# Later modulation vectors as row sums of transposed weights

## The chip, the cores and the metric

The kernel runs on one core of a Trainium2 chip. The core has a matrix engine (TensorE, PE in the profile, with PEld for its weight loads), a vector engine (VectorE, DVE), a scalar engine (ScalarE, ACT), a general engine (GpSimd, POOL) and a queue engine (SyncE, SP) that issues the DMAs here. Time is device microseconds (us) from the first to the last instruction of an execution; lower is better. The kernel before took 1167.83 us in the median of three runs (1166.76 to 1171.36).

## The reference, cut to what matters

A trunk of two layers over 256 latent tokens and 256 context tokens, 1024 wide, in fp32. Each layer mixes tokens (a gated convolution branch beside windowed attention, gated, summed and projected) and then channels (a gated MLP with a short convolution). Both sub-layers are modulated by vectors that depend only on a conditioning vector, one for the latents (`c`) and one for the context (`c_ctx`):

```python
s_lat = jax.nn.silu(c)
s_ctx = jax.nn.silu(c_ctx)
for l in range(DEPTH):
    mod = (s_lat @ w_ada[l] + b_ada[l])[:, None, :]
    sh1, sc1, g1, sh2, sc2, g2 = jnp.split(mod, 6, axis=-1)
    mod_c = s_ctx @ w_ada[l] + b_ada[l]
    ...
    h = modulate(rmsnorm(x, norm1_g[l]), sh1, sc1)
    ...
    x = x + g1 * gated_merge(...)
    h2 = modulate(rmsnorm(x, norm2_g[l]), sh2, sc2)
    x = x + g2 * conv_ffn(h2, ...)
```

`w_ada[l]` has 1024 rows and 6144 columns, 24 MB a layer in fp32. In column tiles of 128 there are 48 a layer: tiles 0 to 7 are the first shift, 8 to 15 the first scale, 16 to 23 the first gate, then the second shift, scale and gate. Both streams need layer 0's tiles and layer 1's first two parts; of layer 1's later 32 tiles only the latents' half is needed, since the context stream ends there.

## The kernel before

Activations stand with channels on the partitions and tokens along the row (`x[k]`, eight tiles of 128 by 512, latents then context). Weights come in units of 128 by 1024 fp32 (512 KB), fetched by SP into a raw buffer (tag `raw`, four in turn, shared by main weights and modulation weights). A main weight unit is split into two fp32r parts that add up to it: ScalarE writes the high part (line 148), VectorE the low part (line 149); each has four buffers. A product of one unit is three TensorE passes per 128 rows (lines 167 to 169, `mm3`). An output tile of 128 by 512 in PSUM is 24 such products in layer 0 for the 1024-row weights, 12 for the 512-row branch weights.

The order of the work is the order in which the program calls it, engine by engine, and a planner may let an instruction that is ready go ahead of one that is not. Work that is not on the main line of products is written as generators: `add_side` enters one into a list, and `slot()`, called in the middle and at the end of each output tile (`group`, lines 171 to 179), advances each of them by one step. Generators in the list are the convolution's taps (line 521), the attention's steps, the layer norm (`layer_norm`), the norms (`norm`), and the making of modulation vectors.

These vectors are made in three ways before the change:

- `ada_now` (line 273): layer 0's first shift and scale, tile by tile at the start, by `ada_products` (line 188): TensorE takes `sil` (silu of both conditioning vectors, padded to 32 columns) as its stationary side and the raw unit as the moving one, 16 matmul records for two units (line 194), with the sums of the four row tiles on four groups of PSUM rows; ScalarE copies them to `ev` (line 202), TensorE transposes them (line 209), VectorE sums them and adds the bias (lines 211, 213).
- `ada_all` (line 215): the same for seven chunks of two column tiles of layer 0, tiles 16 to 29.
- `ada_vector` (line 227): the rest. VectorE multiplies each row tile of a raw unit by the channel's conditioning value and adds it to an accumulator `acc` (lines 257, 259); after eight row tiles TensorE transposes the accumulator in four pieces (line 236), and VectorE sums along the row (line 242) and adds the bias (line 243). Chunks hold two column tiles for both streams (16 VectorE instructions of 256 columns) or four for the latents alone (eight of 512 columns).

They run as side work in this order: `g1` from the end of layer 0's attention on (the five `ada_vector` chunks of tiles 30 to 39, then the seven `ada_all` chunks), which must be done before the second norm of layer 0; `ada_rest` in layer 0's up-projection (tiles 40 to 47, then layer 1's tiles 16 to 47 for the latents); `ad` in layer 0's down-projection (layer 1's tiles 0 to 15 for both streams). Nothing of it runs in layer 1.

Around `g1` the main line is: gate tiles (`gate`, one unit of 24 products each, evacuated by ScalarE), the attention's output branch (line 786, VectorE multiplies with the gates), the convolution's output branch (lines 790 to 793, VectorE forms the gated sum `z` in two parts), and the output projection (`U_WO`), which reads all eight tiles of `z`. The layer norm of the convolution branch runs beside it as side work; GpSimd does two of its additions (lines 747, 748).

At the start TensorE runs products that nobody reads (`busy`, line 123) until the inputs are there. In layer 0's first stage, up to about 62 us, value and gated-linear products alternate with `ada_now` for the next row tile.

Of the kernel before, what the change touches and what calls it, by code (L numbers as in the profile page):

```python
# [8 lines left out]
F32 = mybir.dt.float32  # L9
# [26 lines left out]
# places of the weight units of a layer: [128 rows, 1024] each  # L36
# [8 lines left out]
def trunk(ctx: ExitStack, tc: tile.TileContext, xt, cvec, wall, wada, params, bias_t, rope_t, out):  # L45
# [22 lines left out]
    def tmp(w=512):  # L68
        return tp.tile([P, w], F32, tag="t", bufs=5, name=nm("t"))
# [45 lines left out]
    sil = cp.tile([P, KD, 32], F32, name="sil")  # L115
# [3 lines left out]
    # TensorE's clock is at its full rate once it has been busy for a while: products for nobody until the inputs are there  # L119
# [5 lines left out]
    busy(28)  # L125
# [5 lines left out]
    lastdma = [None]  # L131

    def raw_unit(src):
        r = wp.tile([P, UW], F32, tag="raw", bufs=4, name=nm("raw"))
        lastdma[0] = sp.dma_start(r, src)
        return r

    def wparts(l, u, at=None, cuts=2):
        """The two parts of a unit: their sum is the unit, exactly. The first cut is split, the others by the call."""
        r = wp.tile([P, UW], F32, tag="raw", bufs=4, name=nm("raw"))  # L140
# [30 lines left out]
    def group(ps, ws, xh, xl, c):  # L171
        """One output tile: the sum over the row tiles ws."""
# [27 lines left out]
    def ada_rows(ps):  # L200
        ev = tp.tile([P, S], F32, tag="ev", name=nm("ev"))
# [3 lines left out]
    def ada_sums(l, j, ev):  # L205
        n = slice(j, j + 9, 8) if l == 0 and j < 8 else slice(2 * j, 2 * j + 2)
# [8 lines left out]
    def ada_all(chunks):  # L215
        late = None
        for l, j in chunks:
            ps = ada_products(l, j, "sc")
            if late:
                ada_sums(*late)  # L220
            late = (l, j, ada_rows(ps))
            yield
            yield
        yield
        ada_sums(*late)

    def ada_vector(chunks):
        """Products and sums over the row tiles on the vector engine: chunks of four column tiles for the latents
        alone, or of two for both streams, in steps of so many row tiles."""
        late = None  # L230
        left = 0

        def sums(l, n, m, acc):
            pt = psum("pt")
            for i in range(4):
                pe.transpose(sl(pt, i), sl(acc, i), ident)  # L236
            if m.shape[1] == 4:
                pv, b = pt.rearrange("p (i k) -> p i k", i=4), pr(l, BADA + n, 4)
            else:
                pv = pt.rearrange("p (s i k) -> p i s k", s=2, i=2)  # L240
                b = pr(l, BADA + n, 2).unsqueeze(2).to_broadcast([P, 2, 2])
            dve.tensor_reduce(m, pv, AX.X, ALU.add)
            dve.tensor_tensor(m, m, b, ALU.add)

        for l, j, both, step in chunks:
            acc = tp.tile([P, 512], F32, tag="acc", bufs=2, name=nm("acc"))
            per = 4 if both else 2
            r = None
            for k in range(KD):
                if k % per == 0:  # L250
                    r = raw_unit(wada[l, (8 * j + k) // per])
                i = k % per
                for s in range(1 + both):
# [826 lines left out]
```

## Time and profile before

| quantity | value |
|---|---|
| runs | 1171.36, 1167.83, 1166.76 us (median 1167.83) |
| profiled execution: span | 1167.3 us; its own time is this span, the page gives nothing around it |
| granted TensorE clock | 0.993 on average |
| busy: TensorE, weight loads | 1147.8 us, 984.5 us |
| busy: VectorE, ScalarE, GpSimd | 955.3 us, 555.5 us, 21.3 us |
| fetched from HBM | 185.47 MB |

Lines of groups read: line of the program, engine, operation, what it writes and reads with buffer numbers left out, sizes, count; then the total busy time and the mean in ns of one; then the engine's idle time just before them with what ended it. A busy TensorE is not TensorE at its peak, as its matmuls overlap: the time from one to the next is shorter than the duration of one. Lines of a timeline begin with the start and the duration in us; `xN` behind them merges N in a row. Lines of waits are the waiting engine and line, what it waited for, and then the total in us, the number and the longest. A line of windows is a stretch of the execution with each engine's busy time in it.

### The profile page before, as it was taken

To read this page: it belongs to the slowest core of one execution; us is meant where nothing else is said; L and a number is where in the kernel's file an instruction comes from. 1 tells how busy PE (TensorE), PEld (TensorE's weight loads), DVE (VectorE), ACT (ScalarE), POOL (GpSimd) and SP (SyncE) were. 2 spreads that over 40 slices of the span, in tenths; PEclk is the share of its full clock that TensorE was granted. 3 is DMA by queue.
4 is the path that set the end of the run, shared out by engine and by line. 5 is a ranking of instruction groups with operands and counts; after the bars stand their busy time and mean duration, and the time that the engine had idled before them with its cause. 6 is when DMAs were issued, how large, how long until landed. Compare 5 with 4: busy or idle time off the path is not lost.

```text
span 1167.3 us, 18318 instructions
## 1 busy us (share of the span) xinstructions
PE 1147.8 (98%) x6958; PEld 984.5 (84%) x6958; DVE 955.3 (82%) x1794; ACT 555.5 (48%) x914; POOL 21.3 (2%) x25
## 2 busy tenths in 40 slices
PE   8999999999999999999999999999999999999997
PEld 7677777878679978888888888989788999999997
DVE  4589999979765899898988688789888799988753
ACT  4346767323243444433443222444566667666542
POOL 0000000000000000000000000000000000000000
PEclk9999999999999999999999999999999999999998
DMA  7964434452771354766754346555756364665651
GB/s 270 322 175 131 116 95 120 157 156 69 244 236 55 109 166 159 234 214 221 221 179 151 122 165 209 160 182 187 182 154 165 133 216 140 207 193 185 185 189 55
DMA packets 60248, 199.25 MB, mean 171 GB/s; under 512 B 7168, under 2 KB 8192, under 8 KB 60160
## 3 DMA queue, kind: packets, MB, share of 16 engines
q1 hardware_dynamic: 60160, 198.08, 54.1%
q8 instruction: 55, 0.90, 0.3%
q14 instruction: 33, 0.27, 0.1%
HBM read 185.47 MB, written 1.05 MB: 160 GB/s over the span
## 4 chain that ended last, share of the span: by engine, by line
PE 75%; issue 17%; DMA 3%; DVE 2%; ACT 1%; POOL 0%; SPq 0%; POOLq 0%; DVEq 0%; ACTq 0%
PE main L167 20%; PE main L169 20%; PE main L168 20%; PE po L472 2%; DMA raw<-in_wall 1%; DMA ks<-qk 1%; PE main L573 1%; PE main L575 1%; PE main L574 1%; PE pt L453 1%; PE pt L236 1%; PE sc L167 1%; PE sc L169 1%; PE sc L168 1%; PE pt L334 1%
## 5 line engine op out<-in xcount | busy, mean ns | idle before, releaser
L167 PE MATMUL main<-h,whi 128*128 128x256 f32 (+1 forms) x1328 | 450.9, 340 | 0.9 <-ACT whi L148 0.9
L169 PE MATMUL main<-h,wlo 128*128 128x256 f32 (+1 forms) x1328 | 446.4, 336 | 0.1
L168 PE MATMUL main<-h,whi 128*128 128x256 f32 (+1 forms) x1328 | 444.7, 335 | 0.0
L148 ACT CAST whi<-raw 128x1024 fp32r<-128x1024 f32 (+1 forms) x247 | 255.0, 1035 | 355.9 <-PE main L168 189.2
L149 DVE TENSOR_TENSOR wlo<-raw,whi 128x1024 fp32r<-128x1024 f32 (+1 forms) x247 | 296.5, 1204 | 81.2 <-ACT whi L148 80.0
L167 PEld LDWEIGHTS main<-h,whi 128*128 128x128 f32 x1328 | 250.9, 189 | 31.7 <-issue 4.5
L169 PEld LDWEIGHTS main<-h,wlo 128*128 128x128 f32 x1328 | 251.0, 189 | 28.4 <-DVE wlo L149 0.7
L168 PEld LDWEIGHTS main<-h,whi 128*128 128x128 f32 x1328 | 251.3, 189 | 27.4 <-issue 0.6
L259 DVE SCALAR_TENSOR_TENSOR acc<-raw,sil,acc 128x256 f32<-128x256 f32 (+1 forms) x294 | 141.8, 530 | 1.1
L521 DVE SCALAR_TENSOR_TENSOR cb<-u,par,cb 128x512 f32<-128x512 f32 (+1 forms) x240 | 142.0, 619 | 0.6
L167 PE MATMUL main<-fh,whi 128*128 128x256 f32 (+1 forms) x396 | 127.2, 321 | 0.0
L169 PE MATMUL main<-fh,wlo 128*128 128x256 f32 (+1 forms) x396 | 126.4, 319 | 0.0
L168 PE MATMUL main<-fl,whi 128*128 128x256 f32 (+1 forms) x396 | 126.4, 319 | 0.0
L169 PEld LDWEIGHTS main<-fh,wlo 128*128 128x128 f32 x396 | 74.5, 188 | 5.9
L168 PEld LDWEIGHTS main<-fl,whi 128*128 128x128 f32 x396 | 74.5, 188 | 5.7
L167 PEld LDWEIGHTS main<-fh,whi 128*128 128x128 f32 x396 | 74.5, 188 | 5.7
L858 ACT ACTIVATE t<-main,par 128x512 f32<-128x512 f32 (+1 forms) x82 | 50.7, 667 | 13.6 <-PE main L169 13.5
L859 DVE SCALAR_TENSOR_TENSOR t<-main,par,t 128x510 f32<-128x510 f32 (+1 forms) x82 | 47.5, 614 | 1.9 <-ACT t L858 1.5
L862 DVE SCALAR_TENSOR_TENSOR t<-main,par,t 128x510 f32<-128x510 f32 (+1 forms) x82 | 46.8, 611 | 0.0
L798 DVE SCALAR_TENSOR_TENSOR x<-main,mod,x 128x256 f32<-128x256 f32 x48 | 22.2, 481 | 27.3 <-PE main L169 27.2
L358 ACT ACTIVATE h<-t,mod 128x256 fp32r<-128x256 f32 x56 | 25.3, 501 | 37.1 <-DVE t L357 37.0
L877 ACT CAST fh<-t 128x512 fp32r<-128x512 f32 (+1 forms) x44 | 22.5, 513 | 32.4 <-DVE t L874 31.7
(162 smaller groups left out, 1284.7 us busy)
## 6 DMA issues: line engine op xcount, KB each, us to landing
raw<-in_wall SPq DMA_DIRECT2D x239, 512.0 KB, 4.2
raw<-in_wada SPq DMA_DIRECT2D x96, 512.0 KB, 4.3
ks<-qk SPq DMA_DIRECT2D x32, 256.0 KB, 5.0
bias<-in_bias_t SPq DMA_DIRECT2D x8, 512.0 KB, 4.4
x<-in_xt SPq DMA_DIRECT2D x8, 256.0 KB, 3.9
raw<-in_wall SPq DMA_DIRECT2D x8, 256.0 KB, 5.9
qs<-qk SPq DMA_DIRECT2D x16, 128.0 KB, 2.4
rope<-in_rope_t SPq DMA_DIRECT2D x2, 512.0 KB, 6.0
```

Of the source, the lines that this page charges most:

```text
L148: act.copy(hi[:, c], r[:, c])
L149: dve.tensor_tensor(lo[:, c], r[:, c], hi[:, c].bitcast(F32), ALU.subtract)
L167: pe.matmul(ps, w[0], xh, start=start, stop=False)
L168: pe.matmul(ps, w[0], xl, start=False, stop=False)
L169: pe.matmul(ps, w[1], xh, start=False, stop=stop)
L259: dve.scalar_tensor_tensor(a, w, c, a, ALU.mult, ALU.add)
L358: act.activation(hi[:, c], y[:, c], AF.Identity, bias=b)
L472: pe.matmul(po[i * HD : (i + 1) * HD, c], self.V[kt][:, h * HD : (h + 1) * HD], pts[i][:, kt - kts[0], :], start=kt == kts[0], stop=kt == ...
L521: dve.scalar_tensor_tensor(cb[j], src, w, cb[j], ALU.mult, ALU.add)
L858: act.activation(c, pv_, AF.Identity, bias=pr(l, FDB + t, 1), scale=w[1])
L859: dve.scalar_tensor_tensor(c[:, :, 1:], pv_[:, :, : S - 1], w[0], c[:, :, 1:], ALU.mult, ALU.add)
L862: dve.scalar_tensor_tensor(c[:, :, : S - 1], pv_[:, :, 1:], w[2], c[:, :, : S - 1], ALU.mult, ALU.add)
```

## The change

All later modulation vectors (every tile but layer 0's first 16) are made in one way, `ada_dots`. The weights of these tiles are handed over transposed: a unit is one column tile, its 128 columns on the partitions and all 1024 rows along the row. The conditioning vectors are needed along the row, the same on every partition: at the start TensorE transposes each `sil` column, broadcast to 128 columns, into PSUM (16 transposes, four banks), and VectorE copies the four banks into two tiles `sb[0]` (latents) and `sb[1]` (context), behind the first norm's mean. Then a modulation value is a row sum of a product:

- for the latents, one VectorE instruction over 1024 columns multiplies the raw tile by `sb[0]` and gives the sum (`accum_out`); it writes the product over the raw tile;
- for the context (48 of the 80 tiles), GpSimd multiplies the raw tile by `sb[1]` into `pj` (one buffer), and a ScalarE copy of `pj` with a sum gives the value;
- one small VectorE instruction adds the bias to the tile before (`shift`).

A tile takes two steps of side work: fetch and GpSimd in the first, ScalarE and VectorE in the second. The transposes of accumulators, the accumulators, `ada_all` and `ada_vector` are gone; `ada_now` stays. The 96 fetches of 512 KB stay.

Memory is moved for `sb` and `pj`: the `t` tiles go from five to four, `acc` and `ev` go, `sil` moves into the pool of layer 0's first half, and the raw buffers go from four to three; in layer 1 every fourth raw tile is taken from an extra one-buffer pool in each half, so that there are four again. The banks that receive the broadcast vectors are those that the value products then use.

```diff
-        return tp.tile([P, w], F32, tag="t", bufs=5, name=nm("t"))
+        return tp.tile([P, w], F32, tag="t", bufs=4, name=nm("t"))
...
-    busy(28)
+    busy(8)
+
+    sb = [cp.tile([P, D], F32, name=f"sb{i}") for i in range(2)]
+    across = [psum() for _ in range(4)]
+    for i in range(4):
+        for k in range(4):
+            kk = 4 * (i % 2) + k
+            pe.transpose(sl(across[i], k), sil[:, kk, i // 2 : i // 2 + 1].to_broadcast([P, P]), ident)
+    busy(20)
...
+    def raw_tile():
+        raws[0] += 1
+        if raw_pools and raws[0] % 4 == 0:
+            return raw_pools[-1].tile([P, UW], F32, tag="raw", name=nm("raw"))
+        return wp.tile([P, UW], F32, tag="raw", bufs=3, name=nm("raw"))
...
-    def ada_all(chunks):
...
-    def ada_vector(chunks):
...
+    def shift(l, n, ns):
+        m = mods[l][:, n, :ns]
+        dve.tensor_tensor(m, m, pr(l, BADA + n, 1).to_broadcast([P, ns]), ALU.add)
+
+    def ada_dots(l, tiles, steps):
         late = None
+        for n, both in tiles:
+            r = raw_unit(wada[l, n])
+            if both:
+                pj = tp.tile([P, UW], F32, tag="pj", name=nm("pj"))
+                pool.tensor_tensor(pj, r, sb[1], ALU.mult)
+            yield
+            if late:
+                shift(*late)
+            if both:
+                act.activation(pj, pj, AF.Copy, accum_out=mods[l][:, n, 1:2])
+            dve.scalar_tensor_tensor(r, r, 1.0, sb[0], ALU.mult, ALU.mult, accum_out=mods[l][:, n, 0:1])
+            late = (l, n, 1 + both)
+            for _ in range(steps - 1):
+                yield
         yield
+        shift(*late)
...
                     mid = next(sums)
+                    with tc.issue_after(mid.ins):
+                        for i in range(4):
+                            dve.tensor_copy(sb[i // 2][:, (i % 2) * 512 : (i % 2 + 1) * 512], across[i])
                     nxt = ada_now(0)
...
-                        yield from ada_vector([(0, j, True, 1) for j in range(15, 20)])
-                        yield from ada_all([(0, j) for j in range(8, 15)])
-
-                    g1 = ada_more()
+                    g1 = ada_dots(0, [(n, True) for n in range(16, 40)], 2)
...
-                    yield from ada_vector([
-                        *((0, j, True, 1.3) for j in range(20, 24)),
-                        *((1, j, False, 1.5) for j in range(4, 12)),
-                    ])
+                    yield from ada_dots(0, [(n, True) for n in range(40, 48)], 2)
+                    yield from ada_dots(1, [(n, False) for n in range(16, 48)], 2)
...
-                ad = ada_vector([(1, j, True, 2) for j in range(0, 8)])
+                ad = ada_dots(1, [(n, True) for n in range(0, 16)], 2)
...
-    u = w.reshape(DEPTH, 2, 4, P, 24, S).transpose(0, 4, 1, 3, 2, 5).reshape(DEPTH, 48, P, UW).copy()
+    u = np.ascontiguousarray(w.transpose(0, 2, 1)).reshape(DEPTH, 48, P, UW).copy()
     u[0, :16] = w[0][:, : 2 * D].reshape(2, 4, P, 2, 8, P).transpose(4, 0, 2, 1, 3, 5).reshape(16, P, UW)
-    u[1, 16:] = w[1][:, 2 * D :].reshape(4, 2, P, 8, 512).transpose(3, 0, 2, 1, 4).reshape(32, P, UW)
```

More of the change, by code (lines that the diff above doesn't have):

```diff
@@ L114, in trunk @@
     dve.memset(mhalf, -0.5)
-    sil = cp.tile([P, KD, 32], F32, name="sil")
+    sil = ea0.tile([P, KD, 32], F32, name="sil")
     dve.memset(sil, 0.0)
@@ L227, in ada_vector @@
-    def ada_vector(chunks):
[L230 to L253, printed above, removed]
-                    w = r[:, i * UW // per : (i + 1) * UW // per]
-                    a, c = acc[:, s * S : (s + 1) * S] if both else acc, sil[:, k, s : s + 1]
-                    if k == 0:
-                        dve.tensor_scalar_mul(a, w, c)
-                    else:
-                        dve.scalar_tensor_tensor(a, w, c, a, ALU.mult, ALU.add)
-                left += 1
-                if left >= step:
-                    left -= step
-                    yield
-                    if late and k >= 2:
-                        sums(*late)
-                        late = None
-            n = 2 * j if both else 4 * j
-            late = l, n, mods[l][:, n : n + 2, :] if both else mods[l][:, n : n + 4, 0], acc
-        yield
-        yield
-        sums(*late)
```

35 lines of the change are left out of this document (18 added, 17 removed).

## The prediction

> **What bounds the kernel now.** I read first the page's busy shares, then a table of windows of the profile, then the single rows of the operations that the change touches.
>
> ```profile
> span 1167.3 us, 18318 instructions
> PE 1147.8 (98%) x6958; PEld 984.5 (84%) x6958; DVE 955.3 (82%) x1794; ACT 555.5 (48%) x914; POOL 21.3 (2%) x25
> ```
>
> TensorE is never idle for long, so time that is taken off it comes off the end, as long as the engines that feed it keep up. The feeder to watch is VectorE (DVE): it makes the low part of each weight unit (line 149). The windows show where it has room (after the stretch, each engine's busy time and instructions, the granted clock, the DMA share, GB/s):
>
> ```profile
> core 0: us, PE busy (x) PEld busy (x) DVE busy (x) ACT busy (x) POOL busy (x), PEclk, DMA share, GB/s
> 20.00:62.00 42.00, 40.84 (x256) 27.56 (x254) 23.80 (x59) 16.48 (x32) 0.00 (x0) 1.00 0.89 311
> 189.00:325.00 136.00, 135.09 (x683) 104.83 (x681) 117.19 (x220) 51.26 (x85) 3.35 (x2) 1.00 0.46 145
> 275.00:300.00 25.00, 25.00 (x113) 20.27 (x112) 24.37 (x46) 7.96 (x11) 0.00 (x0) 1.00 0.33 104
> 300.00:325.00 25.00, 24.09 (x163) 15.81 (x162) 17.05 (x39) 7.37 (x13) 0.00 (x0) 1.00 0.80 269
> 440.00:500.00 60.00, 60.00 (x268) 48.63 (x267) 55.68 (x91) 24.30 (x32) 0.00 (x0) 1.00 0.59 193
> ...
> PEld main L169 <- DVE wlo L149: 1.4, 2, 1.0
> ```
>
> From 189 to 325 us, where layer 0's 24 later modulation tiles for both streams are made, VectorE is busy 117.2 of 136 us, and from 275 to 300 it is full. The last line is from the waits of the weight loads between 189 and 345 us: twice they already waited for VectorE's low part, so its lead over TensorE does run out here. This stretch decides the case.
>
> **What TensorE loses.** Each of the 25 VectorE chunks ended in four transposes; seven more chunks were TensorE products. The first two lines are from the chain of waits, the count from the groups, the rest from the timeline of PE:
>
> ```profile
> 235.15 0.23 PE main L169
> ...
> 240.96 0.44 PE pt L236 x4
> ...
> L236 PE MATMUL pt<-ident,acc 128*128 128x128 f32 x100 | 15.0, 272 | 0.0
> ...
> 307.05 0.39 PE L169 MATMUL main<-sh,wlo 128*128 128x512 f32 x1
> 307.37 1.07 PE L194 MATMUL sc<-raw,sil 128*32 128x256 f32 x16
> 308.37 0.44 PE L209 MATMUL pt<-ident,ev 128*128 128x128 f32 x2
> 308.56 0.48 PE L167 MATMUL main<-sh,whi 128*128 128x512 f32 x1
> ```
>
> The 100 transposes are 25 x 0.44 = 11.0 us on the chain. A product chunk takes TensorE from 307.05 to 308.56, less the 0.23 us that a main product has on the chain: 1.28 us, seven times 9.0. Together **20.0 us**. The 16 new transposes at the start lie where nobody needs TensorE: its warming products end at 10.53 and the first real one begins at 10.85 (rows below), and as many warming products stay as fit.
>
> **What VectorE gets.** Per tile now one multiply with row sum over 1024 columns and one small addition of the bias.
>
> ```profile
> L259 DVE SCALAR_TENSOR_TENSOR acc<-raw,sil,acc 128x256 f32<-128x256 f32 x238 | 99.8, 478 | 0.0
> L259 DVE SCALAR_TENSOR_TENSOR acc<-raw,sil,acc 128x512 f32<-128x512 f32 x56 | 42.0, 750 | 1.1
> L243 DVE TENSOR_TENSOR mod<-mod,par 128x4 f32<-128x4 f32 x25 | 3.9, 156 | 0.0
> L418 ACT ACTIVATION_READ_ACCUMULATOR pp<-sc,mx 128x1 f32 x32 | 6.4, 199 | 0.0
> ...
> 249.00 2.85 DVE L259 SCALAR_TENSOR_TENSOR acc<-raw,sil,acc 128x256 f32<-128x256 f32 x7
> ...
> 189.00:325.00 136.00, 3.27 (x10) 1.00 0.46 145
> 189.00:325.00 136.00, 30.47 (x70) 1.00 0.46 145
> 189.00:325.00 136.00, 3.44 (x5) 1.00 0.46 145
> ```
>
> 256 more columns cost 272 ns, so 1024 last 750 + 2 x 272 = 1.29 us; in a row seven instructions of 0.478 take 2.85 us, so each overlaps the next by (3.35 - 2.85) / 6 = 0.08, leaving 1.21. The addition of 0.156 leaves 0.07. A row sum on VectorE is not in this trace; the nearest row is ScalarE's read of its accumulator, 0.20 us, of which some 0.1 is left by the same overlap. Below it could be nothing; above, the case of half rate among the rivals. I take **1.38 us per tile**. The last three lines are what lines 257, 259 and 242 cost VectorE from 189 to 325: 37.2 us go away there, 24 x 1.38 = 33.1 come. By this alone VectorE would need 117.2 - 37.2 + 33.1 = 113.1 us, and TensorE, which loses five transposed chunks (2.2) and five product chunks (6.4) here, 127.4: room of 14.3 us.
>
> **What GpSimd's multiply costs VectorE.** The context stream is multiplied by GpSimd, 48 times 128x1024, and summed by ScalarE. GpSimd now does two such additions a layer, and VectorE's rows beside them show the price (lines of POOL and of DVE, by time; last, the usual duration of line 521):
>
> ```profile
> 165.70 1.51 POOL L747 TENSOR_TENSOR ss<-cb,cb 128x512 f32<-128x512 f32 x1 [151.60 <-DVE cb L521]
> 166.59 1.17 DVE L521 SCALAR_TENSOR_TENSOR cb<-u,par,cb 128x512 f32<-128x512 f32 x1
> ...
> 203.53 2.15 POOL L748 TENSOR_TENSOR ss<-ss,cb 128x512 f32<-128x512 f32 x1 [36.32 <-DVE cb L521]
> 204.44 1.78 DVE L521 SCALAR_TENSOR_TENSOR cb<-u,par,cb 128x512 f32<-128x512 f32 x1
> ...
> 819.80 1.59 POOL L747 TENSOR_TENSOR ss<-cb,cb 128x256 f32<-128x256 f32 x1 [54.59 <-DVE cb L521]
> 820.71 0.97 DVE L521 SCALAR_TENSOR_TENSOR cb<-u,par,cb 128x256 f32<-128x256 f32 x1
> ...
> 866.61 1.99 POOL L748 TENSOR_TENSOR ss<-ss,cb 128x256 f32<-128x256 f32 x1 [45.22 <-DVE cb L521]
> 867.92 0.42 DVE L650 TENSOR_TENSOR t<-main,rope 128x256 f32<-128x256 f32 x1
> ...
> L521 DVE SCALAR_TENSOR_TENSOR cb<-u,par,cb 128x512 f32<-128x512 f32 x120 | 88.9, 755 | 0.1
> L521 DVE SCALAR_TENSOR_TENSOR cb<-u,par,cb 128x256 f32<-128x256 f32 x120 | 53.1, 483 | 0.4
> ```
>
> Beside 512 columns on GpSimd the instruction of VectorE took 1.78 instead of 0.75, beside 256 columns 0.97 instead of 0.48: it stood for 1.03 and 0.49 us. So 1024 columns would hold VectorE 1.03 + 2 x 0.54 = **2.1 us**. It isn't always paid: 0.42 us at 166.59, nothing at 867.92, where VectorE read PSUM. Of the four holds (3.04 us) 1.94 were paid, 64%. Bounds: nothing (all fall beside PSUM reads or idle time) and all. I take 64%, 1.35 us per tile, since the stretch mixes convolution taps (two SBUF inputs) with PSUM readers.
>
> [...]
>
> In the stretch VectorE then needs 113.1 + 24 x 1.35 = 145.5 us against 127.4: **18.1 us** by which TensorE must wait: behind the row sum, which overwrites the raw tile and so waits for GpSimd, stand VectorE's low parts of weights and the gated sums that the output projection reads, and TensorE waits for both. With no hold paid it waits for none, with all 113.1 + 50.4 - 127.4 = 36.1 us.
>
> In the up-projection the eight tiles 40 to 47 come two per pair of column tiles, where VectorE is nearly full already (55.68 of 60 us).
>
> ```profile
> L149 DVE TENSOR_TENSOR wlo<-raw,whi 128x1024 fp32r<-128x1024 f32 x239 | 291.2, 1221 | 80.8 <-ACT whi L148 79.5
> ```
>
> For a pair it has two low parts (1.14 us each without the overlap), four convolution steps of 510 columns (0.67, as line 521 with 512) and two products of 512 columns (0.6, half a low part and a little): 6.2 us, now plus 2 x 2.73 = 11.6 us. TensorE's 48 main products take 48 x 0.23 = 11.0 to 11.2: 0.4 x 4 = 1.6 us, at the bounds nothing and 2.0 x 4 = 8. The 32 tiles for latents alone (2.8 us per pair) fit. In the down-projection a tile comes per 24 products (5.6 us): 1.14 + 2.73 fits.
>
> **Buffers and start.** Layer 0 has three raw buffers for weights instead of four, and the first stage fetches at 311 GB/s.
>
> ```profile
> SPq L135 <- PE po L194: 8.7, 5, 3.7
> raw<-in_wada SPq DMA_DIRECT2D x96, 512.0 KB, 4.3
> ...
> 1.83 8.70 PE L123 MATMUL sc<-ident 128*128 128x128 f32 x56 [1.83 <-POOL ident masks.py:199]
> 10.85 0.38 PE L334 MATMUL pt<-one,ss 128*128 128x1 f32 x2 [0.32 <-DVE ss L320]
> ...
> 16.23 0.17 DVE L211 TENSOR_REDUCE mod<-pt 128x4 f32<-128x16 f32 x1 [2.07 <-PE pt L209]
> ```
>
> From 20 to 62 us SP waited 8.7 us for buffers that line 194 frees before it could fetch the next tile, while TensorE stood 1.2. With a buffer less the worst is fetching at three quarters, 42 / 3 = 14 us; the best is nothing. I take 2, near the loss that TensorE shows. Later, while branch outputs are formed, two tiles and one weight unit pass the three buffers in the 5.6 us of 24 main products. A tile keeps its buffer for the fetch (4.3 us), GpSimd (2.1) and the row sum (1.3), a unit for the fetch and its two parts (some 1.1 each): (2 x 7.7 + 6.5) / 3 = 7.3 us, 1.7 too much. Over the eight units of that time this is 14 us at most; it delays the same low parts as the holds do, so I count the larger of the two, not both. The four copies of the broadcast vectors from PSUM cost at most line 521's 0.75 us each, 3.0; ahead of 16.23 VectorE stands idle for 2.07 us, so that between nothing and 0.9 us of them lies on the path to the first norm. I count it into the 2.
>
> ScalarE's 48 sums (some 1.1 us each) fall on an engine that is busy 48%. Their wait for GpSimd stands ahead of the high parts of weights (line 148), for a few us that the lead covers. The number of fetches stays.
>
> **Sum:** 1167.3 - 20.0 + 18.1 + 1.6 + 2 = 1169.0 us of span. The page shows no time around its span, and it lies 0.5 us under the median of the runs, 1167.83. I forecast **1169 us**: no change, the saving on TensorE eaten by VectorE.
>
> **Rivals.** *The holds are hidden.* The point is 14.3 / 50.4 = 28% paid: below it VectorE keeps up. For it speaks that the tiles start early (line 259 runs from 189 us on) and VectorE is free for 8 us from 300 to 325; against it the full window 275 to 300. Then 1167.3 - 20.0 + 2 = **1149 us**.
>
> *VectorE is the bound throughout (the slower side).* In the stretch from 189 to 325 us each GpSimd multiply is paid in full, since VectorE always has a two-input instruction next. It decides from 60% paid on, where 113.1 + 0.6 x 50.4 - 127.4 = 15.9 us eat what is left of the 20.0 after the other terms. For it speaks 204.44, against it 867.92. Price: 1167.3 - 20.0 + 36.1 + 8 + 2 = **1193 us**.
>
> *The row sum runs at half rate.* Then each of the 80 tiles costs 1024 x 272 / 256 = 1.09 us more: 26 in the stretch, 4 x 2.2 = 9 in the up-projection, 1169 + 35 = **1204 us**. Against it speaks that lines 259 and 521, with two fp32 inputs from SBUF, show no such rate; they have no row sum. [...]
>
> **How the numbers follow.** No change within its band of 1160 to 1176 (45 to 80% paid): 0.40. Holds hidden, up to 1160: 0.32. VectorE the bound, over 1176: 0.20. Half rate 0.06, others 0.02. The measurement can tell 0.5%, 5.8 us. Faster: 0.32 and the low end of the first band, 0.38; slower 0.20 + 0.08 + the high end, 0.34; the same 0.28. The range, **1146 to 1187**, takes in the lower bound, less the 2 us for buffers, and most of the way to the upper. The likeliest case's own range is 1160 to 1176.
>
> **What would show it.** In the changed profile: no rows of transposes of acc, and PE's products of raw with sil only 128, to po; the row sum near 1.29 us on VectorE (2.4 would be half rate); POOL rows of 1024 columns with VectorE instructions stretched by up to 2.1 us beside them; TensorE waiting between 189 and 345 us, above all while branch outputs are formed. If TensorE shows no wait for VectorE there, the forecast is wrong by these 18.1 us. If it waits for DMA into raw instead, the buffers were the price.

## The result, and the profile after

The changed kernel took **1228.4 us** in the median (1224.0 to 1234.3) against 1169.0 for the kernel before (four runs): **1.0522 times, 95% interval 1.0482 to 1.0563**. The forecast of 1169 us and its range of 1146 to 1187 were both wrong, and on the side of the rival in which VectorE is the bound, 35 us beyond that rival's price too. The page's top and its chain of work that ended last, after the change:

```profile
span 1222.2 us, 17944 instructions
PE 1144.8 (94%) x6748; PEld 976.0 (80%) x6748; DVE 944.8 (77%) x1638; ACT 600.5 (49%) x1003; POOL 142.3 (12%) x73
...
PE 34%; issue 23%; DVE 18%; DMA 18%; POOL 5%; ACT 3%; POOLq 0%; DVEq 0%; SPq 0%; ACTq 0%
```

The same line of the chain in the kernel before:

```profile
PE 75%; issue 17%; DMA 3%; DVE 2%; ACT 1%; POOL 0%; SPq 0%; POOLq 0%; DVEq 0%; ACTq 0%
```

No engine got more work that would explain 55 us of span: TensorE and VectorE are both busy for less time than before (1147.8 and 955.3), and GpSimd, which got 121 us more, is busy 12% of the span. What grew is the time in which they wait for one another, so the chain that ends last now runs through VectorE, DMA and GpSimd. The windows that the prediction used, after the change (columns as there: PE, PEld, DVE, ACT, POOL, granted clock, DMA share, GB/s):

```profile
20.00:62.00 42.00, 37.61 (x235) 23.57 (x235) 19.39 (x50) 13.22 (x27) 0.00 (x0) 1.00 0.79 271
189.00:325.00 136.00, 110.32 (x485) 85.86 (x484) 121.77 (x153) 66.47 (x116) 53.72 (x21) 0.91 0.41 129
275.00:300.00 25.00, 4.59 (x20) 3.38 (x18) 20.09 (x25) 13.26 (x22) 15.46 (x7) 0.69 0.49 155
300.00:325.00 25.00, 23.43 (x97) 19.61 (x98) 19.00 (x28) 9.88 (x16) 7.78 (x4) 0.83 0.27 81
440.00:500.00 60.00, 56.29 (x240) 44.31 (x239) 50.49 (x68) 28.50 (x42) 14.68 (x6) 1.00 0.53 165
```

The stretch that was named as deciding, 189 to 325, does lose most: TensorE works 110 of 136 us. But VectorE isn't full in it (122 of 136), and between 275 and 300 us TensorE works 4.6 of 25 us while VectorE still has 5 us to spare. The waits of TensorE, and one of VectorE (waiting engine and line, what it waited for, total us, times, longest):

```profile
PE pt L320 <- DVE ss L306: 22.0, 1, 22.0
PE main L188 <- DVE wlo L168: 13.5, 10, 2.8
PE main L186 <- DVE t L852: 9.6, 11, 2.8
PE main L186 <- ACT whi L167: 7.2, 5, 2.7
PE main L186 <- ACT fh L867: 5.8, 1, 5.8
```

```profile
DVE raw L252 <- POOL pj L246: 69.0, 20, 6.1
```

One wait is 22 us long. TensorE stands at line 320, the small products that sum the layer norm's squares over partitions, and the gate and branch products behind it in its queue can't start. VectorE and GpSimd around it, by time:

```profile
236.64 2.80 POOL L246 TENSOR_TENSOR pj<-raw,sb 128x1024 f32<-128x1024 f32 x1 [6.21 <-DMA raw<-in_wada]
237.09 2.37 DVE L236 TENSOR_TENSOR mod<-mod,par 128x2 f32<-128x2 f32 x1
...
275.64 1.23 DVE L252 SCALAR_TENSOR_TENSOR raw<-raw,sb 128x1024 f32<-128x1024 f32 x1 [3.68 <-POOL pj L246]
...
277.19 2.41 POOL L246 TENSOR_TENSOR pj<-raw,sb 128x1024 f32<-128x1024 f32 x1 [1.59 <-DMA raw<-in_wada]
...
277.76 2.92 DVE L168 TENSOR_TENSOR wlo<-raw,whi 128x1024 fp32r<-128x1024 f32 x1 [0.63 <-ACT whi L167]
...
289.63 1.23 DVE L252 SCALAR_TENSOR_TENSOR raw<-raw,sb 128x1024 f32<-128x1024 f32 x1 [2.23 <-POOL pj L246]
...
290.78 2.48 DVE L742 SCALAR_TENSOR_TENSOR cb<-po,cb 128x512 f32<-128x512 f32 x4
...
294.66 2.35 POOL L246 TENSOR_TENSOR pj<-raw,sb 128x1024 f32<-128x1024 f32 x1 [1.45 <-DMA raw<-in_wada]
294.94 2.61 DVE L306 TENSOR_TENSOR ss<-ss,t 128x512 f32<-128x512 f32 x1 [0.47 <-ACT t L302]
```

Two things are to be seen. First, the **hold**: in these rows a VectorE instruction with two SBUF inputs that starts beside a GpSimd multiply doesn't end before it. The bias addition of two columns (line 236) took 2.37 us (0.15 in the run without context work) and ended with the multiply; a low part took 2.92 (1.22) and an addition of squares 2.61 (0.68), ending 1.08 and 0.54 us after theirs. Line 742, which takes one input from PSUM, wasn't held: its four instructions lasted 683 ns in the mean, 684 in the kernel before, beside a multiply that ran from 290.85 to 293.21. Second, the **order**: the layer norm's next step (line 742) stands in VectorE's queue behind row sums, though its input from TensorE (line 739) was there from about 272 us on, and each row sum stands behind a fetch and a multiply.

### The profile page after: what moved, and what is told of

It is laid out like the page before. It is cut to its first block, busy times and chain, and to the rows that moved or that the text cites. A ratio compares the mean times of both kernels' runs of the same rounds, so it can differ in the third digit from the quotient of the medians.

```text
span 1222.2 us, 17944 instructions
## 1 busy us (share of the span) xinstructions
PE 1144.8 (94%) x6748; PEld 976.0 (80%) x6748; DVE 944.8 (77%) x1638; ACT 600.5 (49%) x1003; POOL 142.3 (12%) x73
## 3 DMA queue, kind: packets, MB, share of 16 engines
HBM read 185.47 MB, written 1.05 MB: 153 GB/s over the span
## 4 chain that ended last, share of the span: by engine, by line
PE 34%; issue 23%; DVE 18%; DMA 18%; POOL 5%; ACT 3%; POOLq 0%; DVEq 0%; SPq 0%; ACTq 0%
DMA raw<-in_wada 14%; PE main L186 8%; PE main L188 8%; PE main L187 8%; POOL pj L246 4%; DVE wlo L168 4%; DVE raw L252 4%; DMA raw<-in_wall 3%; DVE cb L509 3%; ACT whi L167 1%; PE po L458 1%; PE main L561 1%; PE main L563 1%; PE main L562 1%; DVE mod L236 1%
## 5 line engine op out<-in xcount | busy, mean ns | idle before, releaser
L168 DVE TENSOR_TENSOR wlo<-raw,whi 128x1024 fp32r<-128x1024 f32 (+1 forms) x247 | 302.4, 1228 | 71.1 <-ACT whi L167 70.3
L252 DVE SCALAR_TENSOR_TENSOR raw<-raw,sb 128x1024 f32<-128x1024 f32 x80 | 97.6, 1221 | 99.3 <-POOL pj L246 69.0
L246 POOL TENSOR_TENSOR pj<-raw,sb 128x1024 f32<-128x1024 f32 x48 | 121.3, 2527 | 403.7 <-DMA raw<-in_wada 381.4
L509 DVE SCALAR_TENSOR_TENSOR cb<-u,par,cb 128x512 f32<-128x512 f32 (+1 forms) x240 | 151.3, 659 | 0.7
L251 ACT ACTIVATE pj<-pj 128x1024 f32<-128x1024 f32 x48 | 50.9, 1060 | 154.4 <-POOL pj L246 154.4
L861 ACT ACTIVATE t<-t 128x512 f32<-128x512 f32 (+1 forms) x44 | 23.0, 524 | 91.8 <-DVE t L852 91.3
L324 POOL TENSOR_TENSOR rs<-red,mhalf 128x2 f32<-128x2 f32 (+1 forms) x9 | 10.9, 1211 | 394.4 <-DVE red L322 390.0
L849 DVE SCALAR_TENSOR_TENSOR t<-main,par,t 128x510 f32<-128x510 f32 (+1 forms) x82 | 46.7, 612 | 0.4 <-ACT t L848 0.4
```

Of the source, the lines that this page charges most:

```text
L168: dve.tensor_tensor(lo[:, c], r[:, c], hi[:, c].bitcast(F32), ALU.subtract)
L246: pool.tensor_tensor(pj, r, sb[1], ALU.mult)
L251: act.activation(pj, pj, AF.Copy, accum_out=mods[l][:, n, 1:2])
L252: dve.scalar_tensor_tensor(r, r, 1.0, sb[0], ALU.mult, ALU.mult, accum_out=mods[l][:, n, 0:1])
L509: dve.scalar_tensor_tensor(cb[j], src, w, cb[j], ALU.mult, ALU.add)
L849: dve.scalar_tensor_tensor(c[:, :, 1:], pv_[:, :, : S - 1], w[0], c[:, :, 1:], ALU.mult, ALU.add)
```

## The ledger used below

Every kernel here runs the same 5988 main products, in the same order but for some stretches (18 to 195 places, none of them at the rows below), so each can be laid beside the kernel before, product by product. The lag in us behind it, at seven of them, in one profiled execution of each (that of the changed kernel took 1224.0 us and that of the first fills 1172.7, 4 and 7 us under their medians):

```
product  before at  what begins          after  b3   noctx3 noctx4  a4   later later_4 vec4  fills tied_3 tied_4
   0       18.1     first product          0.2   2.5   1.0   0.9    1.5   1.1   0.9  -0.1   7.4   0.6   1.5
 192       75.0     (end of first stage)   5.3   8.0   7.3   2.0    1.7   5.8   0.1  -0.4  13.5   5.0   1.8
 768      246.8     gates, branches        8.1   9.0   7.8   1.5    5.1   6.3  -0.4  -0.9  15.0   5.3   2.2
1344      376.8     (in up-projection)     32.1  12.6  -2.9  -9.2   34.4  31.0  32.0   6.6   3.2   5.4   2.8
2496      631.0     down-projection       44.0  21.4  -2.3 -14.0   35.9  42.2  35.7   3.6   6.1   2.1  -2.3
3264      775.4     (behind it, layer 1)  61.8  24.9  -1.2 -18.7   34.8  59.2  33.7  -0.2   8.1   4.8  -6.8
5987     1157.6     last product          55.2  23.4  -5.3 -22.8   30.5  55.8  29.6  -0.1   3.8   3.7  -6.9
```

b3 to tied_4 are the runs of the next section, in its order, the two mixes and fills on four buffers left out. Hold below means VectorE's busy time above what its instructions, form by form, last in the run without any context work.

## The experiments

**Fewer buffers alone: the kernel before with three raw buffers.**

```diff
-        r = wp.tile([P, UW], F32, tag="raw", bufs=4, name=nm("raw"))
+        r = wp.tile([P, UW], F32, tag="raw", bufs=3, name=nm("raw"))
```

(At both places.)

> The kernel before with three raw buffers instead of four, and nothing else. Theory HOLD (GpSimd's multiplies stop VectorE's two-input instructions, and that is the loss): 1168 to 1174, as only the first stage loses the 5 us seen in the changed kernel. Theory BUFFERS (with three raw buffers every fetch waits for the release of a tile just used, and that is the loss): 1180 to 1210, as the old scheme keeps its raw tiles longer still.

Measured 1194.1 us, 1.0237 (1.0191 to 1.0282) times the kernel before: 27.5 us for one buffer, with nothing else changed. In its ledger, a third of the lag is there by product 192; the rest comes in small pieces, mostly in the two projections. Waits of TensorE for a modulation tile in the first stage, this kernel and the one before:

```profile
PE po L194 <- DMA raw<-in_wada: 4.9, 6, 1.5
```

```profile
PE po L194 <- DMA raw<-in_wada: 0.9, 1, 0.9
```

So the buffer is a real cost by itself, and the prediction's 2 us for it was far too low.

**No context work, three and four buffers.** The multiply and ScalarE's sum are left out (the modulation tiles are filled with zeros at the start, and the context gets the bias alone); VectorE's row sums stay.

```diff
-            if both:
-                pj = tp.tile([P, UW], F32, tag="pj", name=nm("pj"))
-                pool.tensor_tensor(pj, r, sb[1], ALU.mult)
             yield
...
-            if both:
-                act.activation(pj, pj, AF.Copy, accum_out=mods[l][:, n, 1:2])
```

> The changed kernel without the context's values (no GpSimd multiply, no sum on ScalarE; the context's later modulation is the bias alone), still with three raw buffers in layer 0. HOLD: 1150 to 1158, all of the loss but the first stage's 5 us is gone and the 20 us of TensorE show. BUFFERS: 1170 to 1195, as fetch (3.8 us) and row sum (1.3 us) still take turns in three buffers.

> The same without the context's values, with four raw buffers throughout (the product's buffer is free). HOLD: within 6 us of the run with three buffers. BUFFERS: 15 us or more under it, at 1148 to 1155.

Measured 1165.7 us (0.9994, 0.9983 to 1.0006) with three buffers and 1147.5 us (0.9837, 0.9794 to 0.9880) with four. Four buffers and latents alone give 19 us, the prediction's saving of 20.0 us on TensorE, and end 1.5 us from its rival of hidden holds (1149). The row sums are as cheap as it put them. With three buffers 18 of the 19 us are gone again: that gap of 18 us is the one expected of BUFFERS, while 1165.7 itself lies between the two ranges.

**Four buffers and the multiply.** The change with four raw buffers throughout; to make room, `pj` is bf16 in one of the `t` tiles.

```diff
-        return wp.tile([P, UW], F32, tag="raw", bufs=3, name=nm("raw"))
+        return wp.tile([P, UW], F32, tag="raw", bufs=4, name=nm("raw"))
...
-                pj = tp.tile([P, UW], F32, tag="pj", name=nm("pj"))
+                pj = tmp().bitcast(BF16)
```

> The changed kernel with four raw buffers throughout; the room comes from GpSimd's product, which is written in bf16 into one of the four t tiles instead of a tile of its own. BUFFERS is worth what the run without the context's values showed, 18 us, or the 27 of the kernel before with three: 1200 to 1212, with the taps still stretched and the wait of the layer norm's matrix sums still there. If the hold is the smaller part: under 1190.

Measured 1197.6 us, 1.0262 (1.0213 to 1.0312), 2 us under the first range and over the second: the buffer is worth 30.8 us in the changed kernel, nearly all of it in the two projections. Between products 768 and 1344 the lag still grows by 29 us (24 with three).

**A later start: the tiles wait until the convolution's taps are all issued**, first with three buffers, later with four.

```diff
+        while hold():
+            yield
...
-                    g1 = ada_dots(0, [(n, True) for n in range(16, 40)], 2)
+                    g1 = ada_dots(0, [(n, True) for n in range(16, 40)], 2, lambda: taps)
```

> The changed kernel with layer 0's first 24 tiles begun only when the convolution's taps are all issued; nothing else. If the 22 us wait of the layer norm's sums comes from GpSimd stopping the taps: the wait goes, and 10 to 20 of its 28 us come back (1205 to 1220), the rest paid in the branches, where the same 24 holds then fall. If it comes from the buffers: no change, 1222 to 1234.

> Four raw buffers, and the first tiles wait until the convolution's taps are done. Later than the taps with three buffers changed nothing (1224). Theory, the taps are where the hold is dearest, and with three buffers the gain was eaten behind them by the slower passing of tiles while branch outputs are formed: with four buffers the start behind the taps now pays, 1172 to 1190. Rival, the 24 tiles' holds have to be paid in full wherever VectorE is close to full, and behind the taps it is as full as in them: no change against 1198, 1191 to 1206.

Measured 1224.3 (1.0491, 1.0443 to 1.0539) and 1200.6 (1.0303, 1.0276 to 1.0329), no change against 1228.4 and 1197.6. With three buffers I read that as a sign for the buffers; with four the same edit still brought nothing, so that reading fell, and with it my theory that the taps are where the hold is dearest. The ledger says why: at product 768 the late starter on four buffers is level with before (-0.4), at 1344 it lags 32.0. The waits of TensorE in it:

```profile
PE main L189 <- DVE wlo L169: 28.2, 10, 6.8
PE main L187 <- ACT whi L168: 10.0, 3, 7.4
```

The 22 us at the layer norm are gone, and TensorE waits for low parts instead. Of the 24 multiplies 22 now fall between products 768 and 1344 (16 in the changed kernel), and 35.6 us of holds (against 22.8), where TensorE needs each low part and each gated sum at once. In the changed kernel 17.4 us of holds lie between products 192 and 768, beside the taps, and had cost TensorE only 2.5 us by then (against tied_3); the taps that they delayed came due at line 320, as I read it. In both places the holds are paid before 1344.

**No GpSimd: both row sums on VectorE, four buffers.**

```diff
...
-                pool.tensor_tensor(pj, r, sb[1], ALU.mult)
...
-                act.activation(pj, pj, AF.Copy, accum_out=mods[l][:, n, 1:2])
+                junk = tmp().bitcast(BF16)
+                dve.scalar_tensor_tensor(junk, r, 1.0, sb[1], ALU.mult, ALU.mult, accum_out=mods[l][:, n, 1:2])
```

> Both streams' row sums on VectorE (the context's product goes as bf16 into a t tile and is not read), no GpSimd, no ScalarE, four raw buffers. A tile for both costs VectorE 2.6 us where the changed kernel has 1.3 and a hold of 2.1. HOLD and BUFFERS both gone: 20 us less on TensorE, but VectorE needs 80 + 24 x 2.7 = 145 us in the stretch from 189 to 325 us where TensorE has 127, so part of it comes back as a wait: 1152 to 1166. If the hold was not the loss: as with the hold, over 1185.

Measured 1169.4 us, 1.0026 (1.0007 to 1.0045): outside what I expected, and 28 us faster than the multiply on four buffers. GpSimd's help is worth less than nothing: against the run without context, 48 more row sums of 1.22 us on VectorE (58 us) cost 22 us, the engine that was to take them over 50. What keeps this kernel from the 1147 is VectorE itself, nearly full where TensorE waits for it (17.0 us for low parts, under 0.9 in the run without context). The windows of this run, then of the kernel before:

```profile
260.00:330.00 70.00, 54.48 (x222) 42.00 (x221) 65.42 (x121) 19.57 (x26) 2.00 (x1) 0.90 0.48 149
```

```profile
260.00:330.00 70.00, 69.09 (x383) 51.18 (x383) 56.90 (x116) 22.11 (x34) 1.19 (x1) 1.00 0.52 170
```

**Two mixes without GpSimd, four buffers:** 14, or all 24, of the tiles 16 to 39 as TensorE products as before, row sums on VectorE for the rest (in the first stretch in four steps of side work a tile instead of two). The calls alone, first the one with 14, then the other:

```diff
-                    g1 = ada_dots(0, [(n, True) for n in range(16, 40)], 2)
+                    def ada_more():
+                        yield from ada_dots(0, [(n, True) for n in range(30, 40)], 4)
+                        yield from ada_all([(0, j) for j in range(8, 15)])
+
+                    g1 = ada_more()
```

```diff
-                        yield from ada_dots(0, [(n, True) for n in range(30, 40)], 4)
-                        yield from ada_all([(0, j) for j in range(8, 15)])
+                        yield from ada_all([(0, j) for j in range(8, 20)])
```

> As vec4_no_gpsimd, but tiles 16 to 29 of layer 0 stay TensorE's products (ada_all, in the old layout of these units) and only the old VectorE tiles become row sums on VectorE. TensorE loses 100 transposes, 11 us; VectorE has 2.7 us for a tile for both streams where it had 3.4: 1152 to 1160, under the kernel before.

> The mix with all 24 tiles of the first stretch as products of TensorE (12 chunks), and row sums on VectorE for both streams only from tile 40 on; four raw buffers. The mix with 14 of the 24 on TensorE ran 1163.9. Five more chunks on TensorE cost 5 x 1.28 = 6.4 us; VectorE loses 20 row sums (25 us) in a stretch in which the mix still fell 4.2 us behind before. Theory, what the mix lost there was VectorE's work: the two nearly cancel, 1163 to 1168. Rival, the stretch's loss is from fetches and not from VectorE: 1168 to 1172. If VectorE's relief is worth more than the 4.2 us: 1157 to 1162.

Measured 1163.9 us (0.9969, 0.9948 to 0.9990) and 1163.6 us (0.9981, 0.9965 to 0.9997). The first misses its range of 1152 to 1160. Both are a little faster than the kernel before, by less than the 0.5% that I would call a difference, and like each other: five more chunks on TensorE and twenty fewer row sums on VectorE cancel. It is the most of the idea that I found.

**Fills in place of the multiply.** To take away the hold and leave GpSimd its work, the multiply becomes fills, which read nothing (the context's modulation is then not computed). First with three and with four buffers like this:

```diff
-                pool.tensor_tensor(pj, r, sb[1], ALU.mult)
+                pool.memset(r[:, :512], 0.5)
+                pool.memset(pj, 0.5)
+                pool.memset(r[:, 512:], 0.5)
```

(With four buffers: half of the raw tile, the whole of it, then `pj`, which lies in a `t` tile.)

> The changed kernel with three fills in the place of the GpSimd multiply (half the raw tile, the product tile, the other half: some 2 us, behind the same fetch and ahead of the same row sum, with no read of SBUF); the values are wrong. HOLD: the convolution taps go back to 0.75 us and the 22 us wait of the layer norm's matrix sums goes, 1185 to 1200. BUFFERS: 1215 to 1230, since the chain fetch, GpSimd, VectorE in three buffers is as long as before.

> The kernel with four raw buffers and with GpSimd's multiply replaced by fills of the same tiles, about 2 us of GpSimd per tile that read nothing from SBUF (the context's modulation values are wrong by it; ScalarE's sums, VectorE's row sums and the order stay). Theory, the two causes are separate and add up: from after's 1228, 31 off for the buffer (1228 to 1198) and 49 off for the hold (1228 to 1180), 1148, that is 1143 to 1155, near the 1147 of the kernel without any context work on four buffers. Rival, they are one shortage, where a late VectorE keeps the buffers and more buffers cover a late VectorE, so that either cure takes most of the same time away: 1162 to 1178.

Measured 1179.7 us (1.0125, 1.0094 to 1.0156) and 1151.1 us (0.9882, 0.9855 to 0.9909). The first lies under both of its ranges; the second met its number, and buffer and hold seemed to add up. But the ledger shows that the sum came out by accident: with three buffers the first product was already 7.4 us late and product 192 13.5. The timeline at its start:

```profile
12.89 1.06 ACT L253 ACTIVATE pj<-pj 128x1024 f32<-128x1024 f32 x1 [1.04 <-POOL pj L247]
...
14.09 0.95 POOL L247 MEMSET pj<- 128x1024 f32 x1 [1.24 <-ACT pj L253]
```

A fill of `pj` depends on no tile, so the planner moved such fills, with ScalarE's sums behind them, to the start, in the way of the first weights; and with three buffers only 1.05 us of GpSimd then stood between a tile's fetch and its row sum, instead of 2.4. (With four, the first ten sums ran ahead too, from 171 us on, where they delayed no start.) So the fills were tied to their tile and made as long as the multiply:

```diff
-                pool.tensor_tensor(pj, r, sb[1], ALU.mult)
+                first = pool.memset(r[:, :8], 0.5)
+                with tc.issue_after(first.ins):
+                    mid = pool.memset(pj, 0.5)
+                with tc.issue_after(mid.ins):
+                    pool.memset(r, 0.5)
+                    pool.memset(r[:, 512:], 0.5)
```

> Three raw buffers, GpSimd's multiply replaced by fills that are tied to the tile: a few columns of the raw tile, then pj, then the raw tile one and a half times, about 2.5 us in a row like the multiply, and nothing read from SBUF (the context's values are wrong by it). In the first kernel with fills the fill of pj was tied to nothing: the trace shows eleven of the context's sums at its start, where the first product came 7.4 us late, and between the fetch of a tile and its row sum stood 1.05 us of GpSimd instead of 2.4. Theory, the hold is the loss and the time that a tile spends on GpSimd is covered: with the late start gone the 1179.7 fall to 1164 to 1174. Rival, a good part of what the first fills saved was the shorter passing of a tile through three buffers: in the down-projection fetch 3.6, GpSimd 2.4 and row sum 1.25 in turn are 7.3 us for a tile against 5.6 of TensorE, whatever GpSimd does in its part, 16 times 1.7 us: 1180 to 1200.

> The same tied fills with four raw buffers. If a fourth buffer covers the time that a tile spends on GpSimd, no change against the 1151 of the first fills on four buffers: 1146 to 1157, and against the multiply on four buffers (1198) the difference is the hold alone, 41 to 52 us. If the tile's time on GpSimd costs with four buffers too: 1160 to 1175.

Measured **1172.1 us** (1.0027, 1.0004 to 1.0050) with three buffers and **1160.0 us** (0.9946, 0.9925 to 0.9968) with four. GpSimd's groups with three buffers:

```profile
L250 POOL MEMSET raw<- 128x1024 f32 x48 | 45.9, 956 | 0.0
L248 POOL MEMSET pj<- 128x1024 f32 x48 | 45.9, 955 | 5.3 <-ACT pj L256 5.3
L251 POOL MEMSET raw<- 128x512 f32 x48 | 25.3, 527 | 2.6
...
L246 POOL MEMSET raw<- 128x8 f32 x48 | 5.1, 105 | 347.0 <-DMA raw<-in_wada 301.3 <-DVE wlo L168 19.7 <-DVE cb L514 8.6
```

2.54 us of GpSimd per tile (956 + 955 + 527 + 105 ns), as long as the multiply's 2.53, and VectorE isn't held: its two-column additions, in this kernel and then in the changed one:

```profile
L236 DVE TENSOR_TENSOR mod<-mod,par 128x2 f32<-128x2 f32 x48 | 8.5, 178 | 1.4
```

```profile
L236 DVE TENSOR_TENSOR mod<-mod,par 128x2 f32<-128x2 f32 x48 | 26.4, 549 | 1.9
```

The rival, that a tile's turn through three buffers is too slow whatever GpSimd does in it, falls. Between 640 and 740 us, in the down-projection, the changed kernel and then this one:

```profile
640.00:740.00 100.00, 89.38 (x373) 70.75 (x372) 62.00 (x97) 37.76 (x57) 26.92 (x11) 0.97 0.52 158
```

```profile
640.00:740.00 100.00, 100.00 (x491) 83.56 (x490) 56.40 (x98) 42.79 (x63) 30.91 (x51) 1.00 0.58 185
```

TensorE is never idle there with the same fetches, buffers and GpSimd time. With four buffers, though, 1160.0 lies just at the other theory's edge, 9 us over the first fills: there 1.5 us of GpSimd stood between fetch and row sum, here 2.5, and no sum runs ahead of its tile.

One thing differs between the tied fills and the multiply besides the reading: the fill of `pj` ends 1.06 us into the 2.54, so ScalarE's sum can start earlier than behind a multiply. ScalarE waited 83.0 us for GpSimd in all with tied fills and three buffers, 154.4 in the changed kernel. The runs don't separate this from VectorE's hold, so "the hold" below is what the multiply costs beyond fills of the same length.

**Put together** (medians; the kernel before at 1166 to 1167 in these comparisons, at 1169.0 beside the change; the ten runs with tied fills and three buffers lie from 1165.5 to 1174.2):

| kernel | us | step |
|---|---|---|
| row sums, no context, four buffers | 1147.5 | the saving: -19 |
| with GpSimd's time and ScalarE's sums, no hold | 1160.0 | +12.6 |
| with three buffers | 1172.1 | +12.1 |
| with the hold: the change | 1228.4 | +56.3 |

In the other order, on four buffers, the hold costs 1197.6 - 1160.0 = 37.6 us and the buffer then 30.8. Each makes the other dearer by 18.7 us. In the kernels with four buffers and context work `pj` lies in a `t` tile; what that costs isn't separated.

## Why the prediction was wrong, step by step

**What bounds the kernel.** Right that TensorE is the bound as long as it is fed, and that VectorE feeds it.

**TensorE's saving, 20.0 us.** Right: 19 us without context and buffer loss, and the transposes at the start lie where nobody needs TensorE (first product at 18.3 us, before 18.1).

**VectorE's row sum, 1.38 us per tile.** Right. In the groups after the change:

```profile
L252 DVE SCALAR_TENSOR_TENSOR raw<-raw,sb 128x1024 f32<-128x1024 f32 x80 | 97.6, 1221 | 99.3 <-POOL pj L246 69.0 <-DMA raw<-in_wada 30.2
...
L252 DVE DVE_READ_ACCUMULATOR raw<-raw,sb 128x1 f32 x80 | 6.5, 82 | 0.0
```

1.22 us and 0.08 for the accumulator; with the bias addition a turn in a row lasts 1.46 us in the trace (269.27 to 270.73). The half-rate rival is out: a low part of as many columns without a sum takes the same 1.22. Its half rate was a supposition of the prediction's; no run shows it.

**The hold, 2.1 us, 64% of it paid: 18.1 us in the stretch.** The hold and its size were right, the share a little low. VectorE's groups between 189 and 345 us after the change:

```profile
L509 DVE SCALAR_TENSOR_TENSOR cb<-u,par,cb 128x512 f32<-128x512 f32 x43 | 41.9, 990 | 0.1
...
L168 DVE TENSOR_TENSOR wlo<-raw,whi 128x1024 fp32r<-128x1024 f32 x17 | 26.8, 1576 | 2.0 <-ACT whi L167 2.0
L236 DVE TENSOR_TENSOR mod<-mod,par 128x2 f32<-128x2 f32 x22 | 15.9, 721 | 0.5
```

The same in the run without context:

```profile
L168 DVE TENSOR_TENSOR wlo<-raw,whi 128x1024 fp32r<-128x1024 f32 x26 | 31.7, 1219 | 5.1 <-ACT whi L167 5.1
L506 DVE SCALAR_TENSOR_TENSOR cb<-u,par,cb 128x512 f32<-128x512 f32 x42 | 31.4, 770 | 0.1
L238 DVE TENSOR_TENSOR mod<-mod,par 128x2 f32<-128x2 f32 x24 | 3.6, 152 | 0.1
```

These three lines alone are 9.5 + 6.1 + 12.5 us of hold, all forms together 38.3 for 23 multiplies: 1.67 us each, 79% of 2.1. The prediction had 32.4, and its 18.1 us were these less 14.3 us of room. Up to product 1344, the end of that work, the hold cost 26.7 us by the ledger (32.1 of lag in the changed kernel, 5.4 with tied fills; all but 2.8 of it behind product 768): 8.6 more than forecast. The longer holds, 5.9 us more, would make the greater part of that; where the rest comes from stays open. Over the whole program the hold came to 54 us with the multiply and 1.2 with tied fills, which read nothing; even a two-column addition paid nearly the whole time, 2.37 us instead of 0.15.

**The projections, 1.6 and 0 us.** This is where the step failed most. "1.14 + 2.73 fits", said the prediction of the down-projection, and for the up-projection 1.6 with 8 at most: VectorE's sums against TensorE's. Measured against the tied fills, the hold cost 15.2 us between products 1344 and 2496 and 15.1 between 2496 and 3264, though VectorE was held there for only 8.4 and 4.7 us and had room (62 of 100 us busy). With four buffers it was held longer, 14.4 and 19.0 us, and TensorE lost only 6.5 and 3.4. So what is lost there isn't VectorE's time alone but the lead. My reading is that a held low part gives its raw buffer back later, the next fetch starts later, and with three buffers nothing covers it; the runs don't show that chain. How 4.7 us of hold become 15.1 of TensorE I haven't followed wait by wait. Between 675 and 837 us in the changed kernel TensorE's two largest waits are for ScalarE. The first of them ends at 695.69 us, and the timeline before that shows how it came:

```profile
PE main L186 <- ACT fh L867: 5.8, 1, 5.8
PE main L186 <- ACT whi L167: 4.5, 2, 2.7
```

```profile
686.75 1.22 DVE L252 SCALAR_TENSOR_TENSOR raw<-raw,sb 128x1024 f32<-128x1024 f32 x1 [3.91 <-POOL pj L246]
...
691.66 2.83 DVE L864 TENSOR_TENSOR t<-t,t 128x512 f32<-128x512 f32 x1
...
693.98 1.06 ACT L251 ACTIVATE pj<-pj 128x1024 f32<-128x1024 f32 x1 [2.36 <-POOL pj L246]
...
695.04 0.60 ACT L867 CAST fh<-t 128x512 fp32r<-128x512 f32 x1
```

VectorE's steps on this tile (lines 849 and 852, from 687.90 on) stand behind a row sum that waited 3.91 us for a multiply; the product of line 864 is held by the next one (2.83 us, 0.69 with tied fills), and ScalarE's copy of it (line 867) stands behind a sum that waited for that same multiply. Between 675 and 837 us TensorE waits 10.3 us for ScalarE and 7.2 for VectorE, and ScalarE waited 59.5 us for GpSimd's products, against 33.9 in the same work with tied fills. So beside the hold itself the order of the queues takes part here; how the loss is shared stays open, as no run holds the one engine and not the other.

**Buffers and start, 2 us, "the larger of the two, not both".** Wrong twice. The buffer alone costs 12.1 us with tied fills, 18.3 with latents alone, and 27.5 in the kernel before; in the first stage the bound of 14 held (3 to 8 us by product 192). And it isn't the larger of buffer and hold that counts, nor their sum, but more than the sum (12.1 and 37.6 us alone, 68.4 together).

**GpSimd's time and ScalarE's sums, nothing.** Wrong by 12.6 us on four buffers: what "the lead covers" was also counted for nothing. Of these, 3.6 us show already with the first fills, where ScalarE's sums run too (1151.1 against 1147.5).

**The sum.** Of the 53 us between forecast and measured span, 32 are the hold beyond its forecast (8.6 up to product 1344, 13.6 and 15.1 in the projections, less 5.5 behind them) and 21 are buffer, GpSimd's time and ScalarE's sums (the span with tied fills is 1170.8 us, where the forecast without its hold terms is 1149.3). The rival in which VectorE is the bound had the right sign and the wrong place: it let VectorE's sums overrun, while in the trace queues that wait for each other lose the time with VectorE at 77%.

## What to carry to other kernels

An engine's free time in a stretch need not hide a new delay: here 4.7 us of hold, on a VectorE busy for 62 of 100 us, came with 15.1 us lost on TensorE. So price a new stage of a fetch, compute, release loop by the buffers it holds and by what stands behind it in order, besides summing busy times. Elementwise work with two SBUF inputs on GpSimd wasn't free here beside a busy VectorE: doing it on VectorE itself was 28 us faster (1169.4 against 1197.6). And a cause is best taken away with its duration kept: the first fills changed the hold, the time on GpSimd and the start at once, and gave a clean sum by accident.

## What the runs showed that I had not expected

Behind the 22 us wait TensorE's products began 0.43 us apart instead of 0.23. Its timeline (start, duration; the wait stands in brackets):

```profile
301.56 0.59 PE L320 MATMUL pt<-one,ss 128*128 128x1 f32 x2 [21.98 <-DVE ss L306]
...
306.00 0.63 PE L187 MATMUL main<-h,whi 128*128 128x512 f32 x1
306.43 0.63 PE L188 MATMUL main<-h,wlo 128*128 128x512 f32 x1
...
311.58 0.40 PE L186 MATMUL main<-oh,whi 128*128 128x512 f32 x1
311.81 0.39 PE L187 MATMUL main<-ol,whi 128*128 128x512 f32 x1
```

At 306 us one starts every 0.43 us, at 311.6 every 0.23, so some 1.5 us more went behind the wait, by an estimate (7 main products at 0.20 more). This lasted 6.6 us, from 301.56 to the last slow step at 308.13, of which the first 3.4 are line 320's products of one column and only the last 3.1 main products. TensorE's last product before the wait ended at 279.6 us; the granted clock was 1.00 from 280 to 284 us, 0.50 from 285 to 308 and 1.00 again from 309 to 325, and over the whole run it is 0.978 instead of 0.993. What sets these times, one such wait doesn't show.
